# SwiGLU of a decoder layer: 1/(1/rms) made once, the residual divided by whole tiles, operands requested three steps before their split, requests in another order

## The chip, the cores and the metric

The kernel runs on one core of one Trainium2 chip. The metric is the time of one execution on the device in microseconds, as the median of several runs; lower is better. Beside the timed runs there is one execution under the profiler, from which every row below is taken.

## What is computed

The kernel is one inference step of a hybrid decoder layer over 1056 tokens (1024 of a prompt and 8 x 4 sample tokens), model width 1024: a mixing sublayer (mLSTM heads and dilated attention), cross attention over a memory, a SwiGLU feed-forward, a final norm. All is float32. The change touches the feed-forward alone:

```python
def rmsnorm(x, g):
    xf = x.astype(jnp.float32)
    y = xf * lax.rsqrt(jnp.mean(xf * xf, axis=-1, keepdims=True) + EPS)
    return (y * g.astype(jnp.float32)).astype(x.dtype)

def swiglu_ffn(x, g_ffn, w_gate, w_up, w_down):      # D_MODEL 1024, D_FF 2816
    h = rmsnorm(x, g_ffn)
    return x + (jax.nn.silu(h @ w_gate) * (h @ w_up)) @ w_down
```

After it comes `rmsnorm(x, g_final)`. A constant factor of a token cancels in that last norm, which is why the kernel may keep the residual x divided by the SwiGLU norm's factor (`rbc`, the 1/rms of each token on all 128 partitions), in the scale in which the down projection arrives.

## The kernel before, in words

Features lie on partitions, tokens along the free axis: a tile is 128 features x T = 1056 tokens, in two halves of HT = 528 tokens, and a matmul covers QT = 264 of them. The 2816 hidden features are 22 tiles, f = 0 to 21. Tile 0 is computed plainly (`first`). Gate and up of tiles 1 to 21 come from seven products of sums of blocks, P1 to P7, in place of eight (the scheme of Strassen and Winograd); the down projection takes nine pairs of hidden tiles in the same way, as 12 steps of blocks b0 to b11 for three groups of three pairs; the last four hidden tiles go into a plain last stage with the final norm. Each operand is split in two float32r parts, `hi` (a cast, ScalarE) and `lo` (a subtraction, VectorE), and a product is made of three passes: hi by hi, hi by lo, lo by hi. One product is one *step*: 24 matmuls of 128x264 for gate and up (an "a" step), 18 for the down projection (a "b" step).

The steps run in this order: tiles 1 and 2 in turns; tiles 3 to 19 alone, each P1, P6, P5, P7, P2, P3, P4; tiles 20 and 21 in turns; then b0 to b11 by pairs, in turns P1, P6, P2, P5, P7, P3, P4. `product` (L1548 to L1556) issues the matmuls, `aevac` (L1579) reads a finished bank on VectorE or ScalarE and sets it free, `bevac` does so for the b steps.

**Weights.** Raw weights land in 48 pages of 128 columns; an a step needs four of them. `pump` (L1501) requests as many steps ahead as there are free pages, about 12: a load on SyncE's queue, and for some products a second block added by a DMA that accumulates, on GpSimd's queue (L1517). `prepare` (L1534 cast, L1535 subtraction) splits a step's weights four steps before their product and gives the pages back. SyncE's queue runs in the order in which the program is written. The order of the other engines is set by a scheduler when the kernel is built, from what depends on what, and each engine then works through its list in order: what stands behind a waiting instruction waits too.

**The start.** While tile 0 is computed, `xrload` (L1445) loads pairs of tiles of x3T, the residual in DRAM, two buffers in turns, from which the sums of blocks T1 to T4 are made and split (`xsums`).

**Hidden tiles.** The evacuation of P4 ends with L1600, the product of up and gate, and `spill` (L1565) writes sums of each pair of tiles to DRAM (aD, aR) by GpSimd; for an odd tile three of them, made by L1572 to L1575 in three halves of the buffer `cs`. From tile 20 on, `fetch` (L1415) brings them back: it takes two free halves, requests the load on SyncE (L1419), and at once puts the cast (L1420) and the subtraction (L1421) on ScalarE and VectorE. `build` calls it, two per step.

**The residual.** After P5 of each of tiles 3 to 18, `xdivide` (L1640) loads half a row of x3T into the fourth half of `cs`, makes the reciprocal of that half of `rbc` (L1645), multiplies (L1646), and stores to xS. Sixteen calls make eight tiles, which `xsload` reads back for the b steps.

**The end.** When nothing is left to fetch, `last_ready` calls `last_weights` (L1682 load, L1685 cast of 1024 columns) and `last_hidden` (`fetch` from aR) for the four last tiles. The last stage (L1776 on; its matmuls are recorded under the helper's line L267) needs all of these.

Of the kernel before, what the change touches and what calls it, by code (L numbers as in the profile page):

```python
# [138 lines left out]
def body(tc, ctx, I, O):  # L139
# [1240 lines left out]
    late = [(gall, 1024 * more, 0), (gall, 1024 * more, 1), (gall, 1024 * more + T, 0)]  # L1380
    free = {(id(a), o, h): (a, o, h) for a, o in wholes for h in range(2)}

# [4 lines left out]
    def give(x):  # L1387
        free[id(x[0]), x[1], x[2]] = x

    def take_half():  # L1390

        k = min(free, key=lambda k: ((k[0], k[1], 1 - k[2]) in free, k[0] != id(gall), k[1]))
        return free.pop(k)

    def take_whole():
        k = next(k for k in free if k[2] == 0 and (k[0], k[1], 1) in free)
        x = free.pop(k)
        del free[k[0], k[1], 1]
        return x

    give((gx, 5 * T, 0))

    class Op:
# [199 lines left out]
    def first():  # L1603
# [3 lines left out]
        for j, (n0, n) in enumerate(BL):  # L1607
# [22 lines left out]
    usum = [part(ur, 0, HT), part(ur, 1, HT), part(cs, 2, HT), part(cs, 3, HT)]  # L1630
    builds = [(g, p, k) for g in range(NGRP) for p in BY_TURNS for k in range(3)]

    def build(n):

        for _ in range(n):
            if builds and len(free) >= 2:
                g, p, k = builds.pop(0)
                bops.setdefault((g, p), Op(3)).fetch(k, aD[3 * g + k, SPILL[p]])
# [34 lines left out]
    NL = NF - 2 * NPAIR  # L1673
    wl, al = {}, {}

    def last_weights(j):
        run = room(8)
        if run is None:
            return
        raw = at(run)  # L1680
        leave(run)
        sy.dma_start(raw, I["w_down"][j].rearrange("p k c -> p (k c)"))  # L1682
        (a, o, _), (b, o2, _) = take_whole(), take_whole()
        hi, lo = a[:, o:o + 1024], b[:, o2:o2 + 1024]
        act.copy(R(hi), raw)  # L1685
        vec.tensor_tensor(R(lo), raw, hi, ALU.subtract)
        wl[j] = tuple(R(x).rearrange("p (k c) -> p k c", c=P) for x in (hi, lo))

    def last_hidden(j):
        o = al[j] = Op(2)  # L1690
        for h in range(2):
            o.fetch(h, aR[j, :, HT * h:HT * h + HT])

    def last_ready():

        n = len(wl) + len(al)
        wholes_free = sum((k[0], k[1], 1) in free for k in free if k[2] == 0)
        if n < NL:
            if wholes_free >= 2 and not wants:
                last_weights(n)  # L1700
        elif n < 2 * NL and len(free) >= 4:
            last_hidden(n - NL)

# [41 lines left out]
    for s, (kind, i, p) in enumerate(steps):  # L1745
# [3 lines left out]
        if kind == "a":  # L1749
            o = ops[p]  # L1750
            product(bank[kind, i][p], w, o, p in (P2, P3))
            aevac(i, p, bank[kind, i])
            if p == P5 and 3 <= i < 19:
                xdivide(i - 3)
            if i == NF - 2 and p == P1:
                xsload(0), xsload(4), xsload(1)
        else:
            o = bops[g, p]
            product(bank[kind, i][p], w, o, p in (P2, P3, P4))
            bevac(g, q, p, bank[kind, i])  # L1760
            if i == 0 and p == P1:
                xsload(5)
            if i == 0 and p == P2:
                for d in (2, 6, 3, 7):
                    xsload(d)
        if (kind, i) == ("a", NF - 1) or kind == "b" and q == 3:
            o.drop()
        if i >= NF - 2 or kind == "b":
            build(2)
        if not builds:  # L1770
            last_ready()
    while len(wl) + len(al) < 2 * NL:
        last_ready()
    s3, t4 = Ring([stmp[:, 272 * i:272 * i + 272] for i in range(3)]), Ring([ur[:, 272 * i:272 * i + 272] for i in range(3)])
    gbanks = Ring([0, 1, 2])
    for b, (n0, n) in enumerate(FBL):  # L1776
        end = n0 + n == T
        h, o = n0 // HT, slice(n0 % HT, n0 % HT + n)
        for d in range(8):
            pb = gb()  # L1780
            for j in range(NL):
                hi, lo = al[j].ap(h)
                mm(pb[:, :n], wl[j][0][:, d], R(hi[:, o]), j == 0, False)
                mm(pb[:, :n], wl[j][0][:, d], R(lo[:, o]), False, False)
                mm(pb[:, :n], wl[j][1][:, d], R(hi[:, o]), False, j == NL - 1)
            x = xsb[d][:, n0:n0 + n]
# [153 lines left out]
```

## Time and profile before

| | us |
|---|---|
| median of 3 runs | 1765.24 (1763.74 to 1775.59) |
| profiled execution | 1773.3 |
| its span | 1771.5 |
| mean granted TensorE clock over the span | 0.98 |
| TensorE busy | 1688.6 (95% of the span) |
| VectorE / ScalarE / GpSimd busy | 1181.2 / 694.4 / 342.6 |
| SwiGLU products and last stage | from about 1020.6 to the end |

The span runs from the first to the last instruction of that execution; 1.8 us of its time lie around it. A busy time is the sum of an engine's instructions; the granted clock is the share of full speed (2.4 GHz) that the chip allowed TensorE. In the tables of stretches the DMA share is the busy share of the 16 DMA engines, and the last number is GB/s. In lists of waits a line reads: engine and line that waited, what released it, total us, times, longest us. Names are the program's buffers: `f_all` holds the pages and `rbc`, `f_y` holds `cs` and other large buffers, `g_all` and `g_x` the split operands.

### The profile page before, as it was taken

The numbers are of one execution on the slowest core, as the hardware profiler recorded it, in microseconds if no ns is written. First come the engines' busy times: TensorE is split into PE (matmuls) and PEld (weight loads), VectorE is DVE, ScalarE is ACT, GpSimd is POOL, SyncE is SP. The second block draws the span as 40 slices with busy tenths as digits, with TensorE's granted clock in tenths as the row PEclk, the third lists the DMA queues.
The fourth block names the chain that finished last, engine by engine and source line by source line (L and its number), as shares of the span: only waits on it lengthen the run. The fifth ranks groups of instructions, "written<-read, shape, count | busy, mean of one in ns | idle before, by whom it ended". The sixth has DMA issues, their size and how long they took to land. (4 is left out here: it accounts for less than half of the span.)

```text
span 1771.5 us, 32598 instructions
## 1 busy us (share of the span) xinstructions
PE 1688.6 (95%) x12548; PEld 1610.8 (91%) x12548; DVE 1181.2 (67%) x2637; ACT 694.4 (39%) x1401; POOL 342.6 (19%) x440
## 2 busy tenths in 40 slices
PE   6999999999999999999999979999999999999987
PEld 6989999999858999989999979999999999989987
DVE  7786777668628744756644558677677767676666
ACT  6463543533515533434433532222222225344244
POOL 3100101101101323100014212222222221221114
PEclk9999999999999999999999989999999999999998
DMA  5112112122245754474454578777777779998422
GB/s 175 62 34 83 54 53 92 48 65 76 88 157 150 240 174 143 156 265 151 167 158 142 162 208 205 194 199 196 195 199 199 198 216 276 267 236 224 98 87 98
DMA packets 126701, 273.93 MB, mean 155 GB/s; under 512 B 14706, under 2 KB 53010, under 8 KB 126418
## 3 DMA queue, kind: packets, MB, share of 16 engines
q1 hardware_dynamic: 93538, 193.41, 33.8%
q0 software_dynamic: 33008, 78.44, 17.9%
q8 instruction: 99, 1.62, 0.4%
q14 instruction: 56, 0.46, 0.1%
HBM read 204.74 MB, written 51.32 MB: 145 GB/s over the span
## 5 line engine op out<-in xcount | busy, mean ns | idle before, releaser
L267 PE MATMUL banks<-g_all 128*128 128x384 f32 (+6 forms) x4560 | 750.0, 315 | 16.9 <-DVE g_all L422 8.3
L267 PEld LDWEIGHTS banks<-g_all 128*128 128x128 f32 (+1 forms) x4560 | 680.4, 190 | 42.5 <-issue 17.4
L1555 PE MATMUL banks<-g_all 128*128 128x264 f32 x4128 | 583.2, 289 | 33.9 <-DVE f_y L1590 23.9
L1555 PEld LDWEIGHTS banks<-g_all 128*128 128x128 f32 x4128 | 545.6, 193 | 38.7 <-issue 23.0
L1534 ACT CAST g_all<-f_all 128x512 fp32r<-128x512 f32 (+1 forms) x231 | 132.5, 579 | 342.5 <-PE banks L1555 249.3
L1555 PE MATMUL banks<-g_x,g_all 128*128 128x264 f32 x912 | 175.8, 287 | 6.3 <-ACT g_all L1534 5.5
L1535 DVE TENSOR_TENSOR g_all<-f_all,g_all 128x512 fp32r<-128x512 f32 (+1 forms) x231 | 146.0, 637 | 19.3 <-ACT g_all L1534 19.3
L1555 PEld LDWEIGHTS banks<-g_x,g_all 128*128 128x128 f32 x912 | 141.2, 190 | 7.2 <-ACT g_all L1534 5.7
L226 DVE TENSOR_TENSOR g_all<-f_all,g_all 128x1024 fp32r<-128x1024 f32 x88 | 110.3, 1254 | 40.5 <-ACT g_all L225 40.0
L225 ACT CAST g_all<-f_all 128x1024 fp32r<-128x1024 f32 x88 | 91.8, 1047 | 96.2 <-PE banks L267 46.2
L1517 POOL DMA_DIRECT2D f_all<-f_all x66 | 59.6, 908 | 223.2 <-DVE g_all L1535 37.4
L267 PE MATMUL banks<-f_x 128*128 128x129 f32 (+8 forms) x606 | 91.9, 308 | 1.2 <-DVE f_x L733 0.7
L267 PEld LDWEIGHTS banks<-f_x 128*128 128x128 f32 (+4 forms) x606 | 67.4, 160 | 14.8 <-issue 5.7
L267 PE MATMUL banks<-g_y,g_all 128*128 128x384 f32 (+1 forms) x432 | 77.4, 323 | 0.0
L267 PE MATMUL banks<-g_x,g_all 128*128 128x384 f32 (+3 forms) x352 | 75.1, 324 | 0.0
L1128 DVE TENSOR_TENSOR f_all<-banks,f_all 128x384 f32<-128x384 f32 (+1 forms) x48 | 25.1, 523 | 73.8 <-PE banks L267 73.8
L267 PEld LDWEIGHTS banks<-g_y,g_all 128*128 128x128 f32 x432 | 70.4, 188 | 0.0
L1517 POOL DMA_DIRECT2D f_all<-in_w_up_dram x42 | 40.1, 975 | 133.6 <-DMA f_all<-in_w_up_dram 63.5
L267 PEld LDWEIGHTS banks<-g_x,g_all 128*128 128x128 f32 x352 | 60.3, 189 | 0.5 <-issue 0.4
L1421 DVE TENSOR_TENSOR g_all<-g_all 128x528 fp32r<-128x528 f32 x56 | 39.0, 707 | 30.1 <-ACT g_all L1420 29.9
L267 PE MATMUL banks<-f_all 128*32 128x256 f32 (+4 forms) x412 | 43.2, 342 | 14.8 <-DVE f_all L351 4.6
L1420 ACT CAST g_all<-g_all 128x528 fp32r<-128x528 f32 x56 | 35.2, 633 | 52.9 <-DMA g_all<-aD 50.5
(408 smaller groups left out, 2027.0 us busy)
## 6 DMA issues: line engine op xcount, KB each, us to landing
f_all<-in_w_gate_dram SPq DMA_DIRECT2D x105, 256.0 KB, 5.8
f_all<-in_w_down_dram SPq DMA_DIRECT2D x84, 192.0 KB, 4.0
g_all<-aD SPq DMA_DIRECT2D x49, 264.0 KB, 5.1
f_all<-in_w_mq_dram SPq DMA_DIRECT2D x24, 512.0 KB, 4.4
f_all<-in_w_up_dram SPq DMA_DIRECT2D x42, 256.0 KB, 3.5
f_all<-in_w_up_dram POOLq DMA_DIRECT2D x42, 256.0 KB, 6.3
f_all<-f_all POOLq DMA_DIRECT2D x42, 256.0 KB, 4.6
f_all<-in_w_cm_dram SPq DMA_DIRECT2D x20, 512.0 KB, 3.6
```

The source lines that it names most:

```text
L225: act.copy(R(dst_hi), raw)
L226: eng.tensor_tensor(R(dst_lo), raw, dst_hi, ALU.subtract)
L267: pe.matmul(out, l, r, start=start, stop=stop)
L1128: vec.tensor_tensor(x, pb[:, :n], t, ALU.add)
L1420: act.copy(R(hi), lo)
L1421: vec.tensor_tensor(R(lo), lo, hi, ALU.subtract)
L1517: dma.dma_start(at(run).rearrange("p (k c) -> p k c", c=P), src, **how)
L1534: act.copy(R(hi), at(run))
L1535: vec.tensor_tensor(R(lo), at(run), hi, ALU.subtract)
L1555: pe.matmul(o, x[:, k], R(y[:, n]), start=k == 0 and i == 0 and not more, stop=k == K - 1 and i == 2, skip_group_check=more)
```

## The change

- `free`, the list of free halves, becomes first in, first out. `fetch` is split: `load` takes the oldest free half and requests the load on SyncE; `finish`, three steps later at the earliest, takes the half given back last and makes the split. Up to six loads are under way. The operands from aR join the same list, behind those from aD.
- `inverse` makes 1/`rbc` once, in tile 3, in four quarters, and GpSimd stores it to DRAM (invD). In the even tiles 4 to 18, after P5, GpSimd loads all of invD and a whole tile of x3T into `cs` (L1656, L1657), and after P3 VectorE multiplies them into `th` (L1661, 128x1056) and GpSimd stores that to xS (L1662).
- `pump` is called once more in `first`, so that weight requests stand ahead of the last four x3T loads.
- The last weights are requested in the last 14 steps and split, in two chunks of 512 columns, three steps later.

```diff
-    free = {(id(a), o, h): (a, o, h) for a, o in wholes for h in range(2)}
+    free = [(a, o, h) for a, o in wholes for h in range(2)]
...
-    def take_half():
-
-        k = min(free, key=lambda k: ((k[0], k[1], 1 - k[2]) in free, k[0] != id(gall), k[1]))
-        return free.pop(k)
+    def take_half(newest=False):
+        return free.pop(-1 if newest else 0)
...
-        def fetch(self, k, src):
-
-            self.k[k] = (take_half(), take_half())
+        def load(self, k, src):
+
+            self.k[k] = (None, take_half())
+            sy.dma_start(piece(self.k[k][1]), src)
+
+        def finish(self, k):
+
+            self.k[k] = (take_half(True), self.k[k][1])
             hi, lo = (piece(x) for x in self.k[k])
-            sy.dma_start(lo, src)
             act.copy(R(hi), lo)
             vec.tensor_tensor(R(lo), lo, hi, ALU.subtract)
...
                 for b in (stmp.ap, wraw[0]):
                     leave([(b, i) for i in range(16)])
+                pump()
             xsums(j)
...
-    def xdivide(j):
-
-        x, n = part(cs, 3, HT), slice(HT * (j % 2), HT * (j % 2) + HT)
-        sy.dma_start(x, x3T[:, j // 2, n])
-        inv = part(ur, j % 2, HT)
-        vec.reciprocal(inv, rbc[:, n])
-        vec.tensor_tensor(x, x, inv, ALU.mult)
-        gp.dma_start(xS[:, j // 2, n], x)
+    def build(s):
+
+        for _ in range(2):
+            if loaded and loaded[0][0] <= s - 3 and free:
+                loaded[0][1].finish(loaded[0][2])
+                loaded.pop(0)
+        while builds and len(loaded) < 6 and len(free) > len(loaded):
+            name, n, k, (a, b) = builds.pop(0)
+            o = bops.setdefault(name, Op(n))
+            o.load(k, aD[a, b] if name[0] == "b" else aR[a, :, HT * b:HT * b + HT])
+            loaded.append((s, o, k))
+
+    def inverse(j):
+
+        b, n = ((part(cs, 3, HT), part(ur, 0, HT))[j // 2], slice(QT * j, QT * j + QT))
+        o = b[:, QT * (j % 2):QT * (j % 2) + QT]
+        vec.reciprocal(o, rbc[:, n])
+        if j % 2:
+            gp.dma_start(invD[:, HT * (j // 2):HT * (j // 2) + HT], b)
+
+    def xload_by(d):
+        gp.dma_start(part(cs, 0, T), invD)
+        gp.dma_start(part(cs, 1, T), x3T[:, d])
+
+    def xdivide(d):
+
+        vec.tensor_tensor(th.ap, part(cs, 1, T), part(cs, 0, T), ALU.mult)
+        gp.dma_start(xS[:, d], th.ap)
...
+    def last_weights(s):
+
+        if raw_last and raw_last[0][0] <= s - 3 and len(free) >= 4 and not loaded:
+            run = raw_last.pop(0)[1]
...
+                act.copy(R(hi), raw)
+                vec.tensor_tensor(R(lo), raw, hi, ALU.subtract)
...
+                sy.dma_start(at(run), I["w_down"][n].rearrange("p k c -> p (k c)"))
+                raw_last.append((s, run))
...
-            if p == P5 and 3 <= i < 19:
-                xdivide(i - 3)
+            if i == 3 and p in (P6, P5, P7, P2):
+                inverse((P6, P5, P7, P2).index(p))
+            if i % 2 == 0 and 4 <= i < 20:
+                if p == P5:
+                    xload_by((i - 4) // 2)
+                elif p == P3:
+                    xdivide((i - 4) // 2)
...
         if i >= NF - 2 or kind == "b":
-            build(2)
-        if not builds:
-            last_ready()
+            build(s)
+        if s >= len(steps) - 14:
+            last_weights(s)
```

The order on SyncE at the start of the SwiGLU, before: the last weight request that the first free pages allow, the four x3T loads (L1445), and then the requests that follow (L1517).

```order
L1517 DMA f_all_66<-in_w_gate_dram 128x512 [waits DMASW7_49,DMASW3_49,DMAHW5_49,DVE_49,Activation_49]
L1445 DMA f_y_9213<-x3T_78 128x2x1056 [waits DMAHW0_49,DMAHW6_49,DMASW2_49,DVE_49]
L1445 DMA f_y_9213<-x3T_78 128x2x1056 [waits DMAHW7_49,DMAHW1_49,DVE_49]
L1445 DMA f_y_9213<-x3T_78 128x2x1056 [waits DMAHW6_49,DVE_49]
L1445 DMA f_y_9213<-x3T_78 128x2x1056 [waits DMAHW7_49,DVE_49]
L1517 DMA f_all_66<-in_w_up_dram 128x512 [waits DMAHW2_49,Pool_49]
L1517 DMA f_all_66<-in_w_gate_dram 128x512 [waits DMAHW3_49,Pool_49]
```

The same place in the changed kernel, where the x3T loads are L1442 and the requests L1514.

```order
L1514 DMA f_all_66<-in_w_gate_dram 128x512 [waits DMASW7_49,DMASW3_49,DMAHW5_49,DVE_49,Activation_49]
L1514 DMA f_all_66<-in_w_up_dram 128x512 [waits DMAHW6_49,Pool_49]
L1514 DMA f_all_66<-in_w_gate_dram 128x512 [waits DMAHW7_49,Pool_49]
L1514 DMA f_all_66<-in_w_gate_dram 128x512 [waits DMAHW0_49,PE_49,Pool_49]
L1514 DMA f_all_66<-in_w_gate_dram 128x512 [waits DMAHW1_49,PE_49]
L1514 DMA f_all_66<-in_w_gate_dram 128x512 [waits DMAHW2_49]
L1514 DMA f_all_66<-in_w_gate_dram 128x512 [waits DMAHW3_49]
L1514 DMA f_all_66<-in_w_gate_dram 128x512 [waits DMAHW4_49]
L1514 DMA f_all_66<-in_w_gate_dram 128x512 [waits DMAHW5_49]
L1442 DMA f_y_9213<-x3T_78 128x2x1056 [waits DMAHW6_49,DMASW2_49,DVE_49]
L1442 DMA f_y_9213<-x3T_78 128x2x1056 [waits DMAHW7_49,DVE_49]
```

Eight requests have moved ahead of the last four x3T loads. On VectorE in an odd tile before, the multiply by the inverse (L1646, which waits for the x3T load by a DMA's semaphore) stands between the sums of the pair (L1572) and the evacuation of P7 (L1589, L1590):

```order
L1587 TENSOR_TENSOR f_all_66<-banks_65,f_all_66 128x528 [waits PE_49,Activation_49]
L1535 TENSOR_TENSOR g_all_67<-f_all_66,g_all_67 128x512 [waits DMASW7_49,Activation_49]
L1572 TENSOR_TENSOR f_y_9213<-f_y_9213 128x528 [waits DMASW3_49,DVE_49]
L1535 TENSOR_TENSOR g_all_67<-f_all_66,g_all_67 128x512 [waits DMAHW1_49,PE_49,Activation_49]
L1646 TENSOR_TENSOR f_y_9213<-f_y_9213,f_all_66 128x528 [waits DMAHW6_49]
L1589 TENSOR_TENSOR f_y_9213<-f_all_66,banks_65 128x528 [waits DMASW0_49,DVE_49,PE_49]
L1535 TENSOR_TENSOR g_all_67<-f_all_66,g_all_67 128x512 [waits DMAHW2_49,Activation_49]
L1590 TENSOR_TENSOR f_y_9213<-f_y_9213,banks_65 128x528 [waits DVE_49]
```

In the changed kernel the multiply (L1661, which waits for the loads of invD and x3T) stands at the end of an even tile, and the odd tile's evacuations follow; L1585, L1587 and L1588 are L1587, L1589 and L1590 of before, L1598 is L1600, L1532 is L1535.

```order
L1661 TENSOR_TENSOR f_all_66<-f_y_9213 128x1056 [waits DMASW7_49,DMASW0_49,DVE_49]
L1598 TENSOR_TENSOR f_y_9213<-f_all_66,f_y_9213 128x1056
L1532 TENSOR_TENSOR g_all_67<-f_all_66,g_all_67 128x512 [waits DMAHW6_49,PE_49,Activation_49]
L1570 TENSOR_TENSOR f_y_9213<-f_y_9213 128x528 [waits DMASW4_49,DVE_49]
L1585 TENSOR_TENSOR f_all_66<-banks_65,f_all_66 128x528 [waits PE_49,Activation_49]
L1532 TENSOR_TENSOR g_all_67<-f_all_66,g_all_67 128x512 [waits Activation_49]
L1532 TENSOR_TENSOR g_all_67<-f_all_66,g_all_67 128x512 [waits DMAHW0_49,PE_49,Activation_49]
L1587 TENSOR_TENSOR f_y_9213<-f_all_66,banks_65 128x528 [waits DMASW1_49,DVE_49,PE_49]
L1532 TENSOR_TENSOR g_all_67<-f_all_66,g_all_67 128x512 [waits DMAHW1_49,Activation_49]
L1588 TENSOR_TENSOR f_y_9213<-f_y_9213,banks_65 128x528 [waits DVE_49]
```

The multiply has moved from the odd tile's P7 to ten instructions ahead of L1588, and it is one for two. On GpSimd's queue in the changed kernel the loads for it (L1656, L1657) and the store (L1662) stand among the weight accumulations (L1514), the spills (L1575) ahead of them:

```order
L1575 DMA aD_9216<-f_y_9213 128x2x528 [waits DMASW1_49,DVE_49]
L1575 DMA aD_9216<-f_y_9213 128x3x528 [waits DMASW2_49,DVE_49]
L1514 DMA f_all_66<-f_all_66 128x512 [waits DMAHW1_49,DMASW0_49,Activation_49]
L1514 DMA f_all_66<-in_w_up_dram 128x512 [waits DMAHW2_49,DVE_49]
L1656 DMA f_y_9213<-invD_9215 128x1056 [waits DMASW5_49,DMASW2_49]
L1657 DMA f_y_9213<-x3T_78 128x1056 [waits DMASW6_49]
L1514 DMA f_all_66<-f_all_66 128x512 [waits DMASW7_49,DMAHW4_49,DMASW3_49,DVE_49]
L1662 DMA xS_9214<-f_all_66 128x1056 [waits DVE_49]
L1514 DMA f_all_66<-in_w_up_dram 128x512 [waits DMAHW7_49,DMASW1_49,Activation_49]
```

Before, none of the queue's rows was a load for the division (the x3T loads were SyncE's), and each tile had one store of half a row. At the end, ScalarE's list had eight L1420 casts of aR operands directly ahead of the last stage; in the changed kernel the last rows there are L1700 casts of weights and the last L1531, and every L1417 cast stands before them.

## Rows read from the trace of the kernel before

**Rows 1.** Stretches: from:to, length, busy of PE, PEld, DVE, ACT, POOL, PEclk, DMA share, GB/s
```profile
1020.60:1076.20 55.60, 46.20 (x338) 45.34 (x337) 32.35 (x50) 20.24 (x29) 11.16 (x13) 0.91 0.77 206
1076.20:1455.20 379.00, 356.71 (x2858) 355.24 (x2857) 272.38 (x340) 98.24 (x153) 90.28 (x114) 0.98 0.75 202
1455.20:1604.10 148.90, 140.37 (x1095) 137.04 (x1094) 101.22 (x163) 61.69 (x114) 29.43 (x36) 0.98 0.89 250
1604.10:1696.30 92.20, 92.15 (x758) 91.94 (x756) 66.28 (x109) 30.76 (x56) 13.88 (x16) 1.00 0.57 147
1696.30:1771.50 75.20, 57.88 (x432) 55.41 (x432) 46.70 (x157) 36.12 (x77) 28.36 (x35) 0.89 0.27 94
```

**Rows 2.** Timeline of SyncE's queue, 990 to 1040: start, length, line, operation, count
```profile
1000.79 26.00 SPq L1445 DMA_DIRECT2D f_y<-x3T  x4
1026.90 0.54 SPq L1517 DMA_DIRECT2D f_all<-in_w_up_dram  x1
1027.53 6.15 SPq L1517 DMA_DIRECT2D f_all<-in_w_gate_dram  x7
```

**Rows 3.** Timeline of TensorE, 1012 to 1062; in brackets idle before and its releaser
```profile
1032.52 0.75 PE L1555 MATMUL banks<-g_all 128*128 128x264 f32 x4 [2.93 <-ACT g_all L1534]
1045.83 0.59 PE L1555 MATMUL banks<-g_x,g_all 128*128 128x264 f32 x1 [5.46 <-ACT g_all L1534]
```

**Rows 4.** Waits in 1076.2 to 1455.2: total us, times, longest
```profile
DVE f_y L1646 <- DMA f_y<-x3T: 61.0, 16, 4.8
PE banks L1555 <- DVE f_y L1590: 22.3, 8, 4.1
POOL f_all L1517 <- DVE f_y L1572: 18.0, 2, 9.3
```

**Rows 5.** Stretches: tile 5 and tile 6
```profile
1118.80:1144.60 25.80, 22.23 (x171) 22.05 (x170) 17.34 (x22) 6.65 (x10) 4.87 (x6) 0.93 0.67 167
1144.60:1165.00 20.40, 20.40 (x170) 20.40 (x170) 14.65 (x20) 4.98 (x9) 5.52 (x7) 1.00 0.75 219
```

**Rows 6.** Timeline of TensorE, 1128 to 1146
```profile
1137.08 5.05 PE L1555 MATMUL banks<-g_all 128*128 128x264 f32 x27 [3.57 <-DVE f_y L1590]
```

**Rows 7.** Waits in 1455.2 to 1604.1
```profile
ACT g_all L1420 <- DMA g_all<-aD: 41.2, 23, 7.0
```

**Rows 8.** Waits in 1696.2 to 1755
```profile
PE banks L267 <- ACT g_all L1420: 5.3, 2, 4.3
```

**Rows 9.** Lines of VectorE, 1076.2 to 1455.2, by shape: count, busy us, mean ns, idle before
```profile
L1645 DVE RECIPROCAL f_all<-f_all 128x528 f32<-128x528 f32 x16 | 55.2, 3448 | 0.0
L1600 DVE TENSOR_TENSOR f_y<-f_all,f_y 128x1056 f32<-128x1056 f32 x18 | 22.6, 1255 | 0.0
L1646 DVE TENSOR_TENSOR f_y<-f_y,f_all 128x528 f32<-128x528 f32 x16 | 11.4, 710 | 61.0 <-DMA f_y<-x3T 61.0
```

**Rows 10.** Timeline of GpSimd, 1098 to 1146, tile 4 and the next
```profile
1106.90 1.83 POOL L1577 DMA_DIRECT2D aD<-f_y  x2
```

**Rows 11.** DMA issues, 1076.2 to 1455.2: count, KB each, median us to landing
```profile
aD<-f_y POOLq DMA_DIRECT2D x18, 528.0 KB, 6.1
f_all<-in_w_up_dram POOLq DMA_DIRECT2D x35, 256.0 KB, 6.2
f_all<-f_all POOLq DMA_DIRECT2D x35, 256.0 KB, 4.7
f_all<-in_w_up_dram SPq DMA_DIRECT2D x34, 256.0 KB, 3.5
aD<-f_y POOLq DMA_DIRECT2D x9, 792.0 KB, 9.0
```

**Rows 12.** All stores of line L1577, 1076.2 to 1455.2
```profile
DMA to landing us min/median/max: 3.4/7.0/10.8
```

**Rows 13.** DMA issues, 1455.2 to 1604.1
```profile
g_all<-aD SPq DMA_DIRECT2D x36, 264.0 KB, 5.2
```

More of the change, by code (lines that the diff above doesn't have):

```diff
@@ L1387, in give @@
     def give(x):
-        free[id(x[0]), x[1], x[2]] = x
-    def take_half():
-        k = min(free, key=lambda k: ((k[0], k[1], 1 - k[2]) in free, k[0] != id(gall), k[1]))
-        return free.pop(k)
[L1395 to L1399, printed above, removed]
+        free.append(x)
+    def take_half(newest=False):
+        return free.pop(-1 if newest else 0)
     give((gx, 5 * T, 0))
@@ L1559, in body @@
     xS = dram.tile([P, 8, T], F32, name="xS")
+    invD = dram.tile([P, T], F32, name="invD")
     aD = dram.tile([NPAIR, 7, P, HT], F32, name="aD")
@@ L1630, in body @@
     usum = [part(ur, 0, HT), part(ur, 1, HT), part(cs, 2, HT), part(cs, 3, HT)]
[L1631 to L1638, printed above, removed]
-    def xdivide(j):
-        x, n = part(cs, 3, HT), slice(HT * (j % 2), HT * (j % 2) + HT)
-        sy.dma_start(x, x3T[:, j // 2, n])
-        inv = part(ur, j % 2, HT)
-        vec.reciprocal(inv, rbc[:, n])
-        vec.tensor_tensor(x, x, inv, ALU.mult)
-        gp.dma_start(xS[:, j // 2, n], x)
+    builds = [(("b", g, p), 3, k, (3 * g + k, SPILL[p])) for g in range(NGRP) for p in BY_TURNS for k in range(3)]
+    builds += [(("l", j), 2, h, (j, h)) for j in range(NF - 2 * NPAIR) for h in range(2)]
+    loaded = []
+    def build(s):
[20 more added lines that the diff above has]
+        gp.dma_start(xS[:, d], th.ap)
     def xsload(d):
@@ L1673, in body @@
     NL = NF - 2 * NPAIR
[L1674 to L1702, printed above, removed]
+    raw_last, wl = [], []
+    def last_weights(s):
+        if raw_last and raw_last[0][0] <= s - 3 and len(free) >= 4 and not loaded:
+            run = raw_last.pop(0)[1]
+            w = []
+            for c in range(2):
+                hi, lo = take_half(), take_half()
+                hi, lo = piece(hi)[:, :512], piece(lo)[:, :512]
+                raw = at(run)[:, 512 * c:512 * c + 512]
+                act.copy(R(hi), raw)
+                vec.tensor_tensor(R(lo), raw, hi, ALU.subtract)
+                w.append(tuple(R(x).rearrange("p (k c) -> p k c", c=P) for x in (hi, lo)))
+            wl.append(w)
+            leave(run)
+        n = len(wl) + len(raw_last)
+        if not wants and n < NL:
+            run = room(8)
+            if run:
+                sy.dma_start(at(run), I["w_down"][n].rearrange("p k c -> p (k c)"))
+                raw_last.append((s, run))
     def group(kind, order, *tiles):
@@ L1757, in body @@
         else:
-            o = bops[g, p]
+            o = bops["b", g, p]
+            assert None not in o.k and all(x[0] for x in o.k)
             product(bank[kind, i][p], w, o, p in (P2, P3, P4))
@@ L1768, in body @@
         if i >= NF - 2 or kind == "b":
-            build(2)
-        if not builds:
-            last_ready()
-    while len(wl) + len(al) < 2 * NL:
-        last_ready()
+            build(s)
+        if s >= len(steps) - 14:
+            last_weights(s)
+    while len(wl) < NL or loaded or builds:
+        s += 1
+        build(s)
+        last_weights(s)
     s3, t4 = Ring([stmp[:, 272 * i:272 * i + 272] for i in range(3)]), Ring([ur[:, 272 * i:272 * i + 272] for i in range(3)])
@@ L1781, in body @@
             for j in range(NL):
[L1782 to L1785, printed above, removed]
+                hi, lo = bops["l", j].ap(h)
+                wh, wl_ = (w[:, d % 4] for w in wl[j][d // 4])
+                mm(pb[:, :n], wh, R(hi[:, o]), j == 0, False)
+                mm(pb[:, :n], wh, R(lo[:, o]), False, False)
+                mm(pb[:, :n], wl_, R(hi[:, o]), False, j == NL - 1)
             x = xsb[d][:, n0:n0 + n]
```

## The prediction

> **What bounds the kernel now.** I read the stretches of the SwiGLU part first, since the change touches nothing ahead of it. [rows 1] are five of them: products of tiles 1 and 2, tiles 3 to 19, tiles 20 and 21 with b0 to b5, b6 to b11, and the last stage. The fourth is the measure: TensorE is busy for 92.15 of its 92.20 us at granted clock 1.00, so one matmul takes 92.20 / 758 = 0.1216 us. An a step (24 matmuls) is then 2.92 us, a b step (18) 2.19 us, a hidden tile 20.4 us. At this pitch the others lose: tiles 1 and 2 55.6 - 338 x 0.1216 = 14.5 us; tiles 3 to 19 379.0 - 2858 x 0.1216 = 31.5 us; tiles 20 to b5 148.9 - 1095 x 0.1216 = 15.7 us. TensorE sets the time everywhere, and only its waits, with the lower clock behind them, can be won. Then I asked in each stretch who is late.
>
> In tiles 1 and 2 it is weight requests. [rows 2] is SyncE's queue: it stands 26.00 us at the x3T loads (L1445), which wait for buffers, and only behind them, from 1026.90 on, come eight weight requests. In [rows 3] TensorE waits 5.46 us for a split of such weights.
>
> In tiles 3 to 19 TensorE waits 22.3 us in 8 pieces for L1590, and VectorE 61.0 us in 16 pieces at the multiply L1646 for its x3T load [rows 4]. These are one thing: L1646 stands on VectorE just ahead of L1589 and L1590, which set a bank free. [rows 5] is one such tile and the next: tile 5 takes 25.80 us at clock 0.93, tile 6 20.40 at 1.00. In [rows 6] TensorE waits 3.57 us in tile 5. So a stall of 3.57 costs 25.80 - 20.40 = 5.4: the other 1.8 us is matmuls run at the lower of the two clock levels, 1.2 instead of 2.4 GHz.
>
> In tiles 20 to b5 it is ScalarE: 41.2 us in 23 pieces at L1420, the split of operands that come from aD [rows 7]; it stands right behind the request, and the weight splits stand behind it. The last stage begins with a wait of 5.3 us for the same line [rows 8].
>
> **The change part by part**, against the profiled execution (1773.3 us; its span is 1771.5).
>
> *Requests ahead of x3T.* Eight requests pass the four x3T loads on SyncE. In [rows 2] eight issue in 0.54 + 6.15 us, so they are out some 20 us before 1026.90, more than any wait of [rows 3]; the x3T loads move back by at most these 6.7 us, and they wait for buffers anyway. Gain between 0 (something else is as late: the sums from x3T, split after the weights) and 14.5; I take 13.5, with 1 us for those sums.
>
> *The division.* VectorE loses 16 reciprocals (55.2 us) and 16 multiplies (11.4) and gets four quarter reciprocals, by halves 4 x 1.72, and eight multiplies of whole tiles, by L1600's row 8 x 1.26 [rows 9]: 17 us for 67. This work lies beside TensorE's and is worth nothing by itself; the wait counts. SyncE loses 16 x3T loads, which stood among weight requests. GpSimd's queue gets two 540 KB loads (invD, x3T) per even tile instead of nothing, and one store of 540 KB for two of 264. Bytes go up by 8 x 540 KB = 4.3 MB on 202 GB/s x 379 us = 76.6 MB [rows 1], so a DMA share of 0.75 becomes about 0.79.
>
> The new wait: L1661 waits for both loads. In order on VectorE, with L1598, seven shorter ones and L1588 behind it, and L1588 frees the bank for P3 of the odd tile. With t0 the even tile's start, that P3 comes at t0 + 20.4 + 5 x 2.92 = t0 + 35.0. L1661 and L1598 take 1.26 each, the eight others 0.70 [rows 9]: 8.1 us, so L1661 may start at t0 + 26.9 at no cost. When are the loads there? They overwrite the buffer cs, whose last spill to aD goes out near 1107.6 in tile 4, t0 = 1098.3 [rows 10], and lands 9.0 us later [rows 11], at t0 + 18.3. Some 1 us for the two issues, then 1080 KB. Landing bounds from rows: 6.1 us as one 528 KB store [rows 11], and 10.8, the longest of 27 stores [rows 12]: t0 + 25.4 to t0 + 30.1, with 9.0 for the 792 KB store between, t0 + 28.3. So it is close: 0 to 3.2 us of wait in each of eight pairs, 1.4 by the 792 KB row. I take 1 us, since two transfers in flight together are nearer to that row than to the 528 KB one: 8 us stay of 31.5, a gain of 23.5. The Trainium skill (DMA: Bandwidth & Descriptors, "Anatomy of one DMA — SWDGE (gpsimd) path") gives 2.0 us plus bytes / 436e3 for such a transfer, an estimated 3.2 us for 540 KB; the 528 KB row has 6.1. By the page the loads would never be late and the sum would be 8 us lower; I go by the row.
>
> What is behind the waiting instructions: on GpSimd the weight accumulations. It stands about 1 us before invD (the spill) and some 7 before the xS store. Before, its longest stand at an accumulation was 9.3 us [rows 4] and no split was late in that stretch. A request is made 12 steps ahead and split 4 ahead, so it has 8 x 2.92 = 23.4 us, of which load, accumulation and second accumulation take 3.5 + 6.2 + 4.7 = 14.4 [rows 11]. The 9.0 left cover 8. Cost nothing; without the cover it is the third rival.
>
> *Loads three steps ahead of their split.* Three b steps are 6.6 us, the aD load takes 5.2 [rows 13]: most have landed, so ScalarE no longer stands before the weight splits. But the DMA share is 0.89 [rows 1] and the same bytes move. Gain between 0 and 15.7; I take 12.
>
> *The end.* The last weights and operands are now split ahead of the last stage. Gain: the wait of 5.3 [rows 8] and the lower clock behind it, in tile 5's proportion 5.3 x 1.8 / 3.57 = 2.7: 8.0, with bounds of 3 and 10.
>
> Sum: 13.5 + 23.5 + 12 + 8 = 57, so 1773.3 - 57 = 1716.3. The median of the three runs, 1765.24, stands 8.1 below this execution. If the 8.1 are more of the same stalls, the changed kernel ends where it ends; if they lie elsewhere, 8.1 lower. I take half: **1712 us**. With all 69.7 us won and the 8.1 off it is 1695, the lowest that I can justify.
>
> **Rivals.**
> 1. *The x loads land late in every pair*: 10.8 us, so 3.2 us of wait and by tile 5's row 1.8 us of clock, 5.0 x 8 = 40 instead of 8. Speaks for it: more bytes, both loads at once, on a share that is 0.75. Against: the spill is the only large thing then in flight. 1712 + 32 = 1744. The Trainium skill (DMA: Bandwidth & Descriptors, "Issuing engines are not separate DMA queues") says for it that transfers issued by SyncE and GpSimd run on the same 16 engines; the rows show no transfer that was faster for its issuer, 256 KB of w_up take 3.5 us from SyncE and 6.2 accumulated from GpSimd.
> 2. *The stretch to b5 is short of DMA itself*, not of order: share 0.89. Nothing back there: 1724. Against: b6 to b11 run at 0.57 without a loss, so the operands could come earlier.
> 3. *Slower: GpSimd's queue becomes the bound.* If the stands before the xS stores make accumulations late, every pair waits at a split. Point: stands over the 9.0 us of slack. To end above 1783 each pair must lose 71 / 8 = 8.9 us, so stands of 18 us; the rows give 8. A mild form (13 us or more) ends within 1%.
> 4. *The early requests help nothing*, since the sums from x3T are as late: 1726.
>
> **How the numbers follow.** Forecast 0.62 (its own range 1698 to 1723), first rival 0.12, second 0.13, fourth 0.06, third within 1% 0.04, third in full 0.03. The range that holds 8 in 10 takes the forecast, the second and fourth rivals and most of the first: 1696 to 1740. One per cent, about what a measurement of this kernel can tell from no change, is 17.7 us: faster 0.62 + 0.12 + 0.13 + 0.06 = 0.93, same 0.04, slower 0.03.
>
> **What would show it.** In the changed profile: no wait over 1 us of TensorE in the first 56 us of products; at L1661 waits under some 3 us and TensorE's for L1588 near nothing, tiles 3 to 19 in about 355 us; ScalarE's waits for aD loads well under 41 us; the last stage starting without 4 us at L1417. Wrong would be: TensorE waiting for L1531's splits in tiles 3 to 19 (the third rival), or L1661 waiting in every pair with the clock below 0.95 (the first).

## The result, and the profile after

The changed kernel takes 1710.78 us (median of four runs, 1705.53 to 1714.98), against 1767.17 for the kernel before in the runs beside it: a ratio of 0.9673, 95% interval 0.9627 to 0.9718, so some 56 us less. Its profiled execution took 1709.05 us, span 1707.3, 64.2 below the 1773.3 of before.

The same five stretches as in [rows 1], in the changed kernel (columns as there):

```profile
1019.30:1062.20 42.90, 41.42 (x338) 41.02 (x338) 40.19 (x62) 24.11 (x36) 6.64 (x8) 1.00 0.70 194
1062.20:1411.30 349.10, 347.65 (x2859) 347.47 (x2858) 227.05 (x318) 98.81 (x153) 95.28 (x122) 1.00 0.85 232
1411.30:1548.50 137.20, 134.26 (x1094) 133.23 (x1094) 100.12 (x163) 60.97 (x114) 29.63 (x36) 1.00 0.95 272
1548.50:1640.80 92.30, 92.30 (x760) 92.30 (x759) 71.93 (x123) 35.57 (x69) 13.82 (x16) 1.00 0.64 176
1640.80:1707.30 66.50, 54.77 (x432) 53.08 (x430) 40.06 (x147) 30.68 (x68) 28.36 (x35) 0.91 0.20 67
```

By the pitch of 0.1216 us a matmul the loss in each is, before and after:

| stretch | before | after | won | predicted |
|---|---|---|---|---|
| tiles 1 and 2 | 14.5 | 1.8 | 12.7 | 13.5 |
| tiles 3 to 19 | 31.5 | 1.4 | 30.1 | 23.5 |
| tiles 20 and 21, b0 to b5 | 15.7 | 4.2 | 11.5 | 12 |
| last stage, length | 75.2 | 66.5 | 8.7 | 8 |
| sum | | | 63.0 | 57 |

The other 1.2 us are mostly the start of these products, 1019.3 instead of 1020.6; in the runs below it lies anywhere between 1015.8 and 1021.2 and is no effect of the change.

Read the clock column too: it is 1.00 in all four stretches of products. There the work that was done at the lower level went with the waits.

SyncE's queue at the start, which answers to [rows 2]: eight requests are out by about 1001, ahead of the last x3T loads, which take 30.53 us on the queue instead of 26.00. Behind these loads stand only the last two of the fourteen requests of tiles 1 and 2, instead of ten.

```profile
995.73 0.38 SPq L1514 DMA_DIRECT2D f_all<-in_w_up_dram  x1
996.23 4.53 SPq L1514 DMA_DIRECT2D f_all<-in_w_gate_dram  x7
1001.56 30.53 SPq L1442 DMA_DIRECT2D f_y<-x3T  x4
```

Waits in tiles 3 to 19 of the changed kernel, which answer to [rows 4] (engine, line, what released it: total us, times, longest). VectorE still waits for the x3T load, but only one wait of TensorE is left, and it lies in tile 3, ahead of the first such load:

```profile
POOL xS L1662 <- DVE f_all L1661: 40.8, 6, 9.1
DVE f_all L1661 <- DMA f_y<-x3T: 11.8, 7, 3.1
POOL f_y L1656 <- DMA aD<-f_y: 7.3, 6, 2.0
PE banks L1552 <- DVE f_y L1588: 1.4, 1, 1.4
```

Waits of ScalarE for operands in tiles 20 to b5, which answer to [rows 7]: 24.8 us by these three lines instead of 47.6 before (41.2 in [rows 7], and two smaller lines of 5.0 and 1.4).

```profile
ACT g_all L1417 <- DMA g_x<-aD: 11.2, 5, 4.8
ACT g_x L1417 <- DMA g_all<-aD: 7.5, 4, 2.3
ACT g_all L1417 <- DMA g_all<-aD: 6.1, 8, 1.9
```

### The profile page after: what moved, and what is told of

It reads as the page before. It is cut to its first block, busy times and chain, and to the rows that moved or that the text cites. A ratio compares the mean times of both kernels' runs of the same rounds, so it can differ in the third digit from the quotient of the medians.

```text
span 1707.3 us, 32588 instructions
## 1 busy us (share of the span) xinstructions
PE 1665.8 (98%) x12548; PEld 1593.5 (93%) x12548; DVE 1135.9 (67%) x2621; ACT 693.3 (41%) x1405; POOL 349.3 (20%) x450
## 5 line engine op out<-in xcount | busy, mean ns | idle before, releaser
L267 PE MATMUL banks<-g_all 128*128 128x384 f32 (+7 forms) x4424 | 732.9, 315 | 10.4 <-DVE g_all L422 8.4
L267 PEld LDWEIGHTS banks<-g_all 128*128 128x128 f32 (+1 forms) x4424 | 663.1, 190 | 34.9 <-issue 16.9
L1552 PE MATMUL banks<-g_all 128*128 128x264 f32 x4006 | 556.4, 284 | 5.1 <-DVE f_y L1588 1.8
L1552 PEld LDWEIGHTS banks<-g_all 128*128 128x128 f32 x4006 | 519.5, 188 | 6.5 <-DVE g_all L1532 2.4
L1531 ACT CAST g_all<-f_all 128x512 fp32r<-128x512 f32 (+1 forms) x231 | 133.4, 580 | 326.4 <-PE banks L1552 243.9
L1552 PE MATMUL banks<-g_x,g_all 128*128 128x264 f32 x1034 | 196.4, 284 | 0.8 <-DVE g_all L1532 0.8
L1532 DVE TENSOR_TENSOR g_all<-f_all,g_all 128x512 fp32r<-128x512 f32 (+1 forms) x231 | 146.6, 637 | 26.9 <-ACT g_all L1531 26.9
L1552 PEld LDWEIGHTS banks<-g_x,g_all 128*128 128x128 f32 x1034 | 157.6, 188 | 1.0 <-DVE g_all L1532 1.0
L1514 POOL DMA_DIRECT2D f_all<-f_all x66 | 57.8, 876 | 223.1 <-DVE g_all L1532 40.2
L267 PE MATMUL banks<-g_x,g_all 128*128 128x384 f32 (+4 forms) x424 | 89.6, 317 | 0.0
L267 PEld LDWEIGHTS banks<-g_x,g_all 128*128 128x128 f32 x424 | 71.3, 188 | 0.5 <-issue 0.4
L1514 POOL DMA_DIRECT2D f_all<-in_w_up_dram x42 | 39.4, 955 | 72.7 <-DMA f_all<-in_w_up_dram 29.7
L267 PE MATMUL banks<-f_all,f_x 128*64 128x128 f32 (+4 forms) x558 | 49.3, 276 | 0.8 <-DVE f_x L537 0.8
L267 PEld LDWEIGHTS banks<-f_all,f_x 128*64 128x64 f32 (+4 forms) x558 | 37.7, 133 | 12.9 <-issue 5.8
```

The lines of the kernel that those rows point to most:

```text
L267: pe.matmul(out, l, r, start=start, stop=stop)
L1514: dma.dma_start(at(run).rearrange("p (k c) -> p k c", c=P), src, **how)
L1531: act.copy(R(hi), at(run))
L1532: vec.tensor_tensor(R(lo), at(run), hi, ALU.subtract)
L1552: pe.matmul(o, x[:, k], R(y[:, n]), start=k == 0 and i == 0 and not more, stop=k == K - 1 and i == 2, skip_group_check=more)
```

## The experiments

Times are medians beside runs of the kernel before on the same chip. Most of these kernels differ from the changed one by under 1%, near what such times can tell; the stretches of the profile carry the verdicts. Losses are a stretch's length less its matmuls times 0.1216.

### Early weight requests

Early requests undone, all else as in the changed kernel:

```diff
                     leave([(b, i) for i in range(16)])
-                pump()
             xsums(j)
```

> The changed kernel with the early weight requests undone: nothing else differs. Theory (the requests behind the x3T loads were what tiles 1 and 2 waited for): tiles 1 and 2 lose some 14 us again instead of 2.0, TensorE waiting for the cast L1531 in two pieces of about 3 and 5.5 us; all later stretches as in the changed kernel; time about 1722. Rival (the other edits made tiles 1 and 2 faster, the sums from x3T set them): loss stays at 2 to 4 us, time about 1711.

1725.71 us. Tiles 1 and 2, and TensorE's waits there:

```profile
1019.40:1074.80 55.40, 45.69 (x338) 44.85 (x337) 35.53 (x52) 20.25 (x29) 10.74 (x14) 0.91 0.78 211
```

```profile
PE banks L1552 <- ACT g_all L1531: 8.4, 2, 5.4
```

The loss is 14.3 us again, with the two waits and the clock of 0.91 that the kernel before had. This one call is worth the whole term, and the sums from x3T are not what tiles 1 and 2 waited for.

### What the division was worth: work, wait or order

The kernel **before**, with only the x3T load moved up:

```diff
-        sy.dma_start(x, x3T[:, j // 2, n])
...
+    def xload(j):
+        sy.dma_start(part(cs, 3, HT), x3T[:, j // 2, HT * (j % 2):HT * (j % 2) + HT])
...
+            if p == P1 and 3 <= i < 19:
+                xload(i - 3)
             if p == P5 and 3 <= i < 19:
                 xdivide(i - 3)
```

> The kernel before, with the x3T load of each half row requested two steps earlier (after P1 instead of P5); all 16 reciprocals and multiplies stay. Theory (lateness of the load is the loss): VectorE's wait at the multiply falls from 61 us to under 20, tiles 3 to 19 lose 0 to 10 us instead of 31, time about 20 to 30 us below before. Rival (reciprocals and halves are the loss): tiles 3 to 19 still lose 25 us or more. A third way: SyncE now waits for the buffer ahead of weight requests, and TensorE waits for weight splits instead, time as before.

1745.38 us, ratio 0.985 (0.9808 to 0.9892). Tiles 3 to 19, then VectorE's wait at the multiply (L1645 here):

```profile
1075.20:1425.80 350.60, 347.77 (x2858) 347.58 (x2857) 274.74 (x340) 98.94 (x153) 90.64 (x114) 1.00 0.81 218
```

```profile
DVE f_y L1645 <- DMA f_y<-x3T: 4.3, 4, 2.0
```

VectorE does the work of before (274.74 us busy, 272.38 in [rows 1]), and the loss falls from 31.5 to 3.1 us, all of it in tile 3. Two steps of lead for a load win 28.4 us here; the new division won 30.1.

The **changed** kernel with the old division in this form (half rows, 16 reciprocals, no invD):

```diff
-            if i == 3 and p in (P6, P5, P7, P2):
-                inverse((P6, P5, P7, P2).index(p))
-            if i % 2 == 0 and 4 <= i < 20:
-                if p == P5:
-                    xload_by((i - 4) // 2)
-                elif p == P3:
-                    xdivide((i - 4) // 2)
+            if p == P1 and 3 <= i < 19:
+                xload(i - 3)
+            if p == P5 and 3 <= i < 19:
+                xdivide(i - 3)
```

> The changed kernel with the division of before put back (16 half rows, a reciprocal for each), its x3T load requested after P1 instead of P5. Theory (only when the load lands matters; the inverse made once and the whole tiles are worth nothing): tiles 4 to 19 lose 0 to 2 us, time within 4 us of the changed kernel. Rival (the inverse made once gives some of the gain): 8 us or more above it, as when the 16 reciprocals were added to the changed kernel.

1711.19 us (1708.19 to 1713.85), ratio 0.9676 (0.9634 to 0.9719). The changed kernel once more, beside it on the same chip:

> The changed kernel once more, as the measure for the three beside it: about 1711.

1707.76 us (1707.47 to 1709.08), ratio 0.9659 (0.9618 to 0.9700): within these intervals the two are equal. In the profile of the old division tiles 4 to 19 leave no gap:

```profile
1082.70:1409.60 326.90, 326.90 (x2690) 326.90 (x2689) 256.52 (x317) 93.24 (x145) 83.11 (x104) 1.00 0.79 216
```

And the 16 reciprocals added to the changed kernel as work alone:

```diff
+            if p == P5 and 4 <= i < 20:
+                vec.reciprocal(part(ur, (i - 3) % 2, HT), rbc[:, HT * (i % 2):HT * (i % 2) + HT])
```

> The changed kernel with 16 reciprocals of 128x528 put back on VectorE, one after P5 of each of tiles 4 to 19, their results unused. Theory (the gain in tiles 3 to 19 came from the wait that went, not from the work): 16 x 3.45 = 55 us more of VectorE's time, TensorE loses at most 0 to 2 us per pair of tiles, 0 to 12 us in all, tiles 3 to 19 in 349 to 361 us. Rival (VectorE's work itself made the odd tiles late): the loss of before comes back, about 31 us, tiles 3 to 19 in about 380 us.

1722.82 us. Tiles 3 to 19 lose 9.0 us, within the theory's 0 to 12; then the waits, and VectorE at the start of tile 4 (t0 = 1082.2; the added reciprocal is L1764):

```profile
1060.90:1417.60 356.70, 349.96 (x2859) 348.13 (x2858) 277.07 (x334) 98.78 (x153) 95.21 (x122) 1.00 0.83 226
```

```profile
DVE f_all L1661 <- DMA f_y<-x3T: 20.3, 8, 4.4
PE banks L1552 <- DVE g_all L1532: 6.0, 6, 2.6
```

```profile
1081.35 3.45 DVE L1764 RECIPROCAL f_all<-f_all 128x528 f32<-128x528 f32 x1
1087.04 1.25 DVE L1598 TENSOR_TENSOR f_y<-f_all,f_y 128x1056 f32<-128x1056 f32 x1
```

VectorE's busy time in tiles 3 to 19 is about that of the old division in the changed kernel (277.07 us here, 274.75 there), which lost nothing in tiles 4 to 19, so it is not the amount of work. It is where a reciprocal stands: at the end of a tile, ahead of the evacuations of P3 and P4 (L1595 to L1598). L1598 then starts 4.8 us after t0, the start of the even tile, instead of 2.6; the spill of the pair before goes out later; and the loads that overwrite the spill's buffer are issued 17.7 to 19.3 us after t0 instead of 13.8 to 17.0. The multiply starts at 26.5 to 29.1 us, and TensorE waits for a weight split that stands behind it on VectorE (L1532): in all eight pairs the odd tile loses the multiply's start less 26.2, to within 0.1 us. The old division in the changed kernel also has a reciprocal at that place, and loses nothing by it: its x3T load goes into the fourth half of `cs`, which no spill uses, and so does not wait for the spill.

### The price of a late load

The load of the inverse made twice, the second time behind the first:

```diff
     def xload_by(d):
+        gp.dma_start(part(cs, 0, T), invD)
         gp.dma_start(part(cs, 0, T), invD)
```

> The changed kernel with the load of the inverse made twice, the second behind the first: the multiply gets its operands some 7 us later, at about 32 us after the even tile's start, against the 26.9 that the prediction's sum allows. Theory (the first rival of the prediction, with its deadline): each of eight pairs waits about 5 us of TensorE's time, with up to 1.8 us more for the lower clock, 40 to 55 us in all, time about 1750 to 1765. Rival (there is more slack than that sum says): under 1 us per pair, time as the changed kernel.

1722.78 us, far from the 1750 to 1765 of the theory. Tiles 4 to 19, and two of them, tiles 6 and 7:

```profile
1088.70:1423.40 334.70, 328.43 (x2691) 327.29 (x2690) 208.67 (x295) 93.20 (x145) 92.71 (x121) 1.00 0.86 236
1130.60:1151.10 20.50, 20.50 (x171) 20.50 (x169) 13.16 (x19) 5.85 (x10) 6.91 (x9) 1.00 0.97 264
1151.10:1174.10 23.00, 20.92 (x170) 20.52 (x169) 12.92 (x18) 5.82 (x10) 4.63 (x6) 1.00 0.74 196
```

VectorE at the multiply in that pair (L1662 here), on the timeline:

```profile
1160.75 1.26 DVE L1662 TENSOR_TENSOR f_all<-f_y 128x1056 f32<-128x1056 f32 x1 [6.98 <-DMA f_y<-invD]
```

The mechanism is the prediction's, its size is not. Over the eight pairs the multiply starts, after the even tile's start, and the odd tile loses, in us:

| multiply at | 25.7 | 26.3 | 27.0 | 27.2 | 28.6 | 29.2 | 29.9 | 30.1 |
|---|---|---|---|---|---|---|---|---|
| odd tile loses | 0 | 0 | 0 | 0 | 1.05 | 1.64 | 2.41 | 2.56 |

So loss = start - 27.5, and nothing below that, for VectorE's list as it is in this kernel. The deadline reckoned from rows, 26.9, was 0.6 early: from the start of the multiply to the end of L1588 this pair takes 7.3 us, where the sum had 8.1, since the shorter instructions behind L1598, about 0.70 long each, start 0.60 to 0.62 apart. And the second load lands not 7 but 4.2 to 6.7 us after its issue, so lateness is 0 to 2.6 us and not 5. No clock piece comes on top here: the clock stays at 1.00 in tiles 4 to 19.

### The queue that carries the loads

The two loads issued by SyncE instead of GpSimd:

```diff
     def xload_by(d):
-        gp.dma_start(part(cs, 0, T), invD)
-        gp.dma_start(part(cs, 1, T), x3T[:, d])
+        sy.dma_start(part(cs, 0, T), invD)
+        sy.dma_start(part(cs, 1, T), x3T[:, d])
```

> The changed kernel with the loads of the inverse and of x3T issued by SyncE instead of GpSimd, at the same place in the program; SyncE runs in written order, so it stands until the spill that used the buffer has landed, some 7 to 9 us per pair, with weight requests behind it. Theory (a request has about 9 us to spare): TensorE loses 0 to 2 us per pair, time within 16 us above the changed kernel. Rival (a hold of the request queue counts in full): 5 us or more per pair, time above 1750. Second rival (nothing depends on the queue): no loss at all.

1708.09 us. SyncE's queue in tile 4 of this kernel: nothing is issued between the end of the requests at 1092.28 and 1099.13, where it waits for the spill.

```profile
1088.88 3.40 SPq L1514 DMA_DIRECT2D f_all<-in_w_gate_dram  x2
1099.13 0.33 SPq L1656 DMA_DIRECT2D f_y<-invD  x1
```

```profile
1084.40:1411.40 327.00, 327.00 (x2691) 327.00 (x2690) 209.58 (x295) 93.17 (x145) 78.97 (x97) 1.00 0.83 230
```

Tiles 4 to 19 lose nothing, which both the theory (0 to 2 us per pair) and the second rival allow; the first rival falls. SyncE stands 5.6 to 7.8 us per pair, which stays within the 9.0 us of slack that the prediction reckoned, and TensorE loses nothing by the choice of queue at this size. The x3T loads land sooner here, 4.4 to 6.8 us after their issue instead of 6.6 to 9.3; no run shows why.

### The lead between load and split

No lead, at most two loads at a time, as before (first); one step (second); four steps and eight loads (third); four and seven (fourth):

```diff
-            if loaded and loaded[0][0] <= s - 3 and free:
+            if loaded and loaded[0][0] <= s and free:
```

```diff
-            if loaded and loaded[0][0] <= s - 3 and free:
+            if loaded and loaded[0][0] <= s - 1 and free:
```

```diff
-            if loaded and loaded[0][0] <= s - 3 and free:
+            if loaded and loaded[0][0] <= s - 4 and free:
...
-        while builds and len(loaded) < 6 and len(free) > len(loaded):
+        while builds and len(loaded) < 8 and len(free) > len(loaded):
```

The first also requests its loads ahead of that line in the same call, two at most; the fourth has 7 in place of 8.

> The changed kernel with each load from aD and aR split in the same step in which it is requested, at most two at a time, as before; the order in which free halves are taken and all else stay. Theory (ScalarE standing at loads ahead of weight splits was the loss of tiles 20 to b5): ScalarE waits 35 us or more for these loads in that stretch, TensorE loses 12 to 16 us there instead of 4.3, time about 1720. Rival (supply: the DMA engines are busy 0.95 of that stretch, the lead is worth nothing): loss stays at 4 to 6 us.

> The changed kernel with the split one step behind its load instead of three (2.2 us instead of 6.6), up to six loads under way as before. A load takes 5.2 us, so theory (lead against landing time) expects ScalarE to wait some 3 us per load less often than at once: TensorE loses 6 to 12 us in tiles 20 to b5. Rival (the six loads under way do the work, the distance does not matter): 4 us, as in the changed kernel.

> The changed kernel with the split four steps behind its load and up to eight loads under way. Theory (what is left in tiles 20 to b5, 4.3 us, is still loads landing late): 2 to 4 us lost. Rival (it is the DMA engines' limit): 4 us or more, since more loads compete with the weights.

> The changed kernel with the split four steps behind its load and up to seven loads under way. Theory (four steps and a few more loads only just help): tiles 20 to b5 lose 2 to 4 us instead of 4.3, time 0 to 3 us below the changed kernel. Rival (the DMA engines are the limit there): 4 us or more, no gain.

Times: 1722.14, 1717.99, 1709.37 and 1711.88 us. Tiles 20 to b5, one row of each, in that order:

```profile
1414.30:1563.20 148.90, 138.31 (x1095) 135.54 (x1094) 100.78 (x163) 61.84 (x114) 29.60 (x36) 0.99 0.88 250
```

```profile
1410.80:1558.10 147.30, 139.06 (x1094) 136.70 (x1093) 101.38 (x163) 62.73 (x114) 29.62 (x36) 0.98 0.91 256
```

```profile
1410.70:1548.30 137.60, 135.14 (x1093) 134.61 (x1093) 99.92 (x163) 60.10 (x114) 29.64 (x36) 0.99 0.93 271
```

```profile
1416.60:1555.10 138.50, 135.28 (x1094) 134.66 (x1093) 100.01 (x163) 60.42 (x114) 29.58 (x36) 0.99 0.93 269
```

The losses are 15.7 at no lead (before: 15.7), 14.3 at one step, 4.2 at three (the changed kernel), 4.7 and 5.5 at four. With three steps and nothing else changed in this stretch, the other profiles here lose 3.4 to 7.6; the changed kernel once more loses 5.9:

```profile
1408.40:1547.30 138.90, 134.76 (x1094) 133.31 (x1093) 99.76 (x163) 60.90 (x114) 29.55 (x35) 1.00 0.94 269
```

In the first kernel ScalarE waits 47.4 us for these loads, in three lines of which the largest is

```profile
ACT g_all L1417 <- DMA g_all<-aD: 26.8, 16, 5.9
```

One step is 2.2 us, less than the 5.2 us in which a load lands [rows 13], three are 6.6: the gain comes between. It is the order, not a shortage of transfer: the same bytes went in 148.9 us at a DMA share of 0.88 and in 137.2 at 0.95. The first kernel takes its halves in the changed order and still loses what the kernel before lost, so the order of the halves is not what won. Four steps lie within the spread of three: more lead brings nothing that these profiles can tell. One step lost more than the theory's 6 to 12, nearly as much as no lead at all. The two kernels with four steps missed the theory's 2 to 4: tiles 20 to b3 lose under 1 us, and b4 and b5 lose 4.5 to 4.8. That is the rival's number; whether its reason, the DMA engines' limit, makes that piece stays open. No version measured here beats the changed kernel by more than its own two medians differ (1707.76 and 1710.78).

### The last weights

Split in the step of their request:

```diff
-        if raw_last and raw_last[0][0] <= s - 3 and len(free) >= 4 and not loaded:
+        if raw_last and len(free) >= 4 and not loaded:
```

with the request ahead of that line, one block at a time.

> The changed kernel with each of the four last weight blocks split in the step in which it is requested, instead of three steps later; the request still starts 14 steps ahead of the end. Theory (the distance from request to split matters at the end): ScalarE waits some 4 us at each of the four, weight splits stand behind it, TensorE loses 3 to 10 us in b8 to b11 and at the start of the last stage. Rival (starting 14 steps ahead is enough, splits of b steps are made four steps ahead and cover 4 us): nothing lost, time as the changed kernel.

1713.13 us. Waits from b10 on:

```profile
ACT g_x L1706 <- DMA f_all<-in_w_down_dram: 4.5, 2, 3.3
ACT g_all L1706 <- DMA f_all<-in_w_down_dram: 4.3, 1, 4.3
PE banks L267 <- ACT g_all L1706: 0.6, 1, 0.6
```

ScalarE waits 8.8 us and TensorE 0.6. That these splits begin 14 steps ahead of the end is enough; the three steps between request and split are worth about that 0.6. (Its time, 2.4 above 1710.78, holds a loss of 5.4 in tile 3, of which more below.)

## Why the prediction was right, and where it was not

**Time.** 1712 was forecast, 1710.78 came. That it is this close is luck: two errors cancel. The sum gave 57 us where the stretches won 63.0. And half of the 8.1 us between the profiled execution and the median was taken off; the changed kernel's profiled execution is not above its median (1709.05 against 1710.78), and the median of before became 1767.17 with more runs, so that 6.1 of those 8.1 stand. The profiled execution itself was put at 1716.3 and came 7.2 lower.

**Tiles 1 and 2.** Right in mechanism and size, 13.5 against 12.7 (undone: the loss is 14.3 again). The 1 us kept for the sums is there too, as a wait of 1.1 us for L1532 in tile 2, among the splits of those sums on VectorE.

**Tiles 3 to 19.** The mechanism is right, the residual was mis-sized: 8 us were kept for eight late multiplies, and none was late for TensorE. Two numbers in its sum failed: the deadline, by the 0.6 us above, and, above all, the time at which the loads go out. They were put at t0 + 18.3 to t0 + 19.3; in the changed kernel the first is issued 13.8 to 17.0 us after the even tile's start, the second 15.5 to 17.6. In tile 4 (t0 = 1084.3) the spill goes out at 1091.42 and not 8.6 us after t0 as in [rows 10], and the first load is issued at 1099.69. GpSimd on the timeline there:

```profile
1091.42 1.83 POOL L1575 DMA_DIRECT2D aD<-f_y  x2
1099.69 0.56 POOL L1656 DMA_DIRECT2D f_y<-invD  x1 [2.02 <-DMA aD<-f_y]
1110.51 0.56 POOL L1662 DMA_DIRECT2D xS<-f_all  x1 [4.95 <-DVE f_all L1661]
```

The spill waits for the product of up and gate (L1600 before, L1598 now). Before, a reciprocal stands ahead of it on VectorE at the start of tile 4 (t0 = 1098.3), and the product starts at t0 + 4.8; in the changed kernel (second fence) it starts at t0 + 2.6. So it is in all eight pairs of either:

```profile
1097.42 3.45 DVE L1645 RECIPROCAL f_all<-f_all 128x528 f32<-128x528 f32 x1
1103.10 1.26 DVE L1600 TENSOR_TENSOR f_y<-f_all,f_y 128x1056 f32<-128x1056 f32 x1
```

```profile
1086.92 1.25 DVE L1598 TENSOR_TENSOR f_y<-f_all,f_y 128x1056 f32<-128x1056 f32 x1
```

So the spill's time was read from a trace in which the division's own work, which the change takes out, delayed it. The stalls of the odd tiles are not the reason: the kernel before with the early load has none in tiles 4 to 19, and its spill in tile 4 (t0 = 1098.8) still goes out 8.6 us after t0:

```profile
1107.37 1.84 POOL L1577 DMA_DIRECT2D aD<-f_y  x2
```

With the 16 reciprocals put back the loads are issued at t0 + 17.7 to 19.3, about where the sum put them, and tiles 4 to 19 take 335.4 us, 8.5 more than without a gap, against the 8 of the sum (though TensorE waits there for a weight split and not for L1588). The sum is nearly right for the change with the reciprocals left where they were.

The landing was estimated well, at 9.0 us for both loads, against these rows of the DMA issues in tiles 3 to 19 of the changed kernel:

```profile
f_y<-invD POOLq DMA_DIRECT2D x8, 528.0 KB, 7.2
f_y<-x3T POOLq DMA_DIRECT2D x8, 528.0 KB, 8.2
```

The formula of the Trainium skill (DMA: Bandwidth & Descriptors, "Anatomy of one DMA — SWDGE (gpsimd) path") gave an estimated 3.2 us for one of them; the measurement decides. Its conclusion, no wait, held for another reason: the earlier issue. The multiply then starts 23.5 to 26.2 us after t0, ahead of the measured deadline of 27.5.

What is left, 1.4 us, lies in tile 3, in no term of the sum: VectorE waits at L1570 for a spill to land, before it may overwrite that buffer, with L1588 behind it. The same wait is 2.42 us in the kernel before. It varies from run to run: tile 3 loses 0.9 to 6.4 us in the kernels here. In the profile of the kernel with four steps and seven loads it is 5.6, with 4.6 us of that wait and the clock at 0.93:

```profile
1063.60:1089.60 26.00, 22.17 (x170) 21.98 (x169) 16.99 (x23) 5.72 (x9) 8.27 (x11) 0.93 0.88 235
```

**That the division's work is worth nothing by itself** is shown as far as its amount goes, by the old division in the changed kernel and by the early load in the kernel before: the 45 us that VectorE works less in tiles 3 to 19 (272.38 to 227.05) are not in the time. But its place in VectorE's order was worth something, which the prediction left out: with loads that overwrite the spill's buffer, the reciprocals that went were worth 7.6 us (9.0 against 1.4).

**Tiles 20 to b5.** 12 against 11.5 (9.8 by the second profile of the changed kernel), and the lead is what did it.

**The end.** 8 against 8.7, and in its two parts: the wait of 5.3 us for L1420 is gone, and TensorE's busy time in the last stage falls from 57.88 to 54.77 us at a granted clock of 0.91 instead of 0.89, which is 3.1 us for the 2.7 reckoned as lower clock. The three steps between request and split are not what did it, since the kernel without them in the last weights waits only 0.6 us more, and the kernel at no lead, whose operands from aR are split at once, ends in 66.21 us. That it is enough to start ahead of the last stage follows from before and after; no run here starts late again.

**The rivals.** The first, late x loads, is a real mechanism at the measured rate of 1 us for each us beyond t0 + 27.5 (26.2 with the reciprocals back), and it does not occur here. Its remark that the rows show no transfer faster for its issuer compared loads of different kinds; the same x3T loads landed in 6.4 us (median) from SyncE and 8.2 from GpSimd. The second, that nothing comes back in tiles 20 to b5 for shortage of DMA, is refuted by the runs on lead. The third, GpSimd's queue, did not come: it stood up to 9.1 us at the xS store, and with the doubled load another 6 or so at that load, and in neither kernel did TensorE's matmuls wait for a split in tiles 4 to 19 for more than 0.7 us at a time. The fourth is refuted by undoing the requests.

## What to carry to other kernels

Where an engine that works in order waits for a load and the bottleneck waits for what stands behind it, first move the request and not the work: two steps of lead for one load brought 28.4 us where a new algorithm for the division brought 30.1, and three steps between a load and its split brought 11.5 (9.8 in a second profile). Before pricing a new wait, ask which of its inputs are late only because of work that goes, and what stands ahead of them in an engine's order. And measure a deadline by delaying its input on purpose: eight pairs of one run gave it to within some tenths of a us, for that order of the instructions and no other (27.5 and 26.2 here).

## What was not expected of the hardware

In tiles 4 to 19 of the kernel with the doubled load TensorE's waits, at most 1.4 us each in tiles that lose up to 2.6, came without a lower clock (1.00 over 334.7 us), and so did the single wait of 2.6 us in tile 19 of the kernel with the reciprocals:

```profile
1394.30:1417.60 23.30, 20.70 (x170) 20.49 (x170) 14.85 (x18) 5.83 (x10) 5.48 (x8) 1.00 0.83 221
```

The wait of 3.57 us in [rows 6] was followed by a lower clock (0.93 over the tile). Also, the DMA engines kept a share of 0.95 over 137 us, at 272 GB/s, while TensorE lost only 4.2 us; the same bytes at a share of 0.88 came with a loss of 15.7. A share near 1 did not by itself mean that TensorE waits for the DMA engines.
